# Recurrence of a hybrid attention and RWKV-7 step: another order of ready and late work, key transposes parted from their copies, a solve in five pieces, and bulk loads issued by ScalarE

## The chip, the cores and the metric

The kernel runs on one core of one Trainium2 chip. The metric is the device time of one execution in microseconds, as the median of several runs. Of one more execution there is a profile, taken by the hardware profiler; all rows of the trace that are shown here come from it.

## The reference

One step of a decoder with two layers. Layer 0 is sliding-window attention with sinks, layer 1 is RWKV-7 time mixing. 16 learned meta tokens stand ahead of a prompt of 2048 tokens; eight short samples of four tokens go through the same layers from cached states. The change touches the second layer's recurrence and what follows it. For each head, with a 64x64 state S:

```python
def step(S, inp):
    r_t, w_t, k_t, v_t, a_t, b_t = inp
    sa = jnp.einsum('bhvk,bhk->bhv', S, a_t)
    S = S * w_t[:, :, None, :] + sa[..., None] * b_t[:, :, None, :] + v_t[..., None] * k_t[:, :, None, :]
    return S, jnp.einsum('bhvk,bhk->bhv', S, r_t)
...
y = ((y - mean) * lax.rsqrt(var + GN_EPS)).reshape(B, T, R_WIDTH)
y = y * ln_g.astype(f32) + ln_b.astype(f32)
y = (y + bonus.reshape(B, T, R_WIDTH)) * jax.nn.silu(g.astype(f32))
out = jnp.einsum('btw,wd->btd', y.astype(xn.dtype), w_out)
```

mean and var are those of each head's 64 outputs (a group norm). h + out goes through a last RMS norm and is the result. There are 16 heads.

## The kernel before

The attention comes first, then the projections of the second layer, whose results (decayed r, a, k, b, v and a few small vectors) are written to DRAM. The recurrence is the last third of the time, from about 1640 us on. Its tokens are cut into units: unit 0 holds the meta tokens, units 1 to 16 hold 128 prompt tokens each, in four chunks of 32. The recurrence inside a chunk is solved as a small triangular system, so that only chunks follow one another.

What is done for one chunk (`chain`): TensorE (PE) multiplies L (the a and r vectors, loaded from ar) with Z (the state, and under it the chunk's u and v rows) into C; ScalarE (ACT) copies the upper part to R0s; PE multiplies R0s with TT, the inverse of the chunk's triangular matrix; ACT writes the result, u, into Z; PE multiplies Z with LS (transposed keys) into C, and VectorE (DVE) scales that with the decay pe into the next chunk's Z. That is the only chain through the whole recurrence; its instructions are in rows such as `C<-Z,L`, `R0s<-C`, `C<-R0s,TT`, `Z<-C` and `Z<-C,pe`.

Work for other units is laid around that chain by `steady`, which runs for units 2 to 14. With u the current unit:

- Two units ahead (s): `scores` multiplies BK (keys and b) with L into PSUM pz (`pz<-L,BK`). ACT copies a part of it to LAs, DVE masks the rest into L (`L<-pz,smk`). LAs goes to DRAM (`la_d<-LAs`) and comes back in another layout as LA.
- `inverse`: from LA, GpSimd (POOL) builds X, the triangular inverse, in 31 steps of two operations (`XT<-LA,X`, `X<-X,XT`), with four pieces of steps laid between other work. X goes to DRAM (`tt_d<-X`) and comes back as TT. Units 1 and 2 have their solve on DVE.
- `keys`: PE transposes BK into PSUM kt, ACT copies it to LS (eight copies).
- One unit behind: the group norm of the outputs Y (mean, squares `Y<-ytm`, var, `ytm<-ytm,var`, lng, lnb, then vt, the bonus), then `gate` (pd, gt, transposes yps, yp).
- Two units behind: `project_out` (`po<-wo,yp`), the residual h, the sum of squares, ms on POOL, and the store `out_y_prompt`.

These are generators: `run` lets one go on up to a MARK or for a budget of estimated microseconds. DVE, ACT and POOL are held to the order in which the program states their instructions (`in_order` ties each to the one before). On PE, and on the DMA queue of SyncE (SP), a scheduler places them by priority, between anchors. In the kernel before, every load and store of the recurrence is issued by SP, whose queue is first in, first out: what waits at its head holds all behind it. BK has four buffers (two per unit), L six (two per unit), LAs one, X and LA two each, TT one per parity of the unit, h and ytm one.

The bulk loads of unit s are: BK, two transfers of 512 KB, and four transfers of L, of 256 KB each. They are issued in the first chunk (BK, and L's first half unless it was loaded already), in the second (L's second half) and in the fourth (the first half of the unit after s).

Of the kernel before, what the change touches and what calls it, by code (L numbers as in the profile page):

```python
# [19 lines left out]
P = 128  # L20
# [10 lines left out]
def tile_hybrid_step(ctx: ExitStack, tc: tile.TileContext, a, o, c):  # L31
# [16 lines left out]

    def dma(out, in_):
        return nc.sync.dma_start(out=out, in_=in_).ins  # L50

# [819 lines left out]

    idle = lambda: iter(())
    PRE = min(3, len(units) - 1)
    nbuf = {"L": 6, "BK": 4, "Z": 4}
# [13 lines left out]

    def load_BK(u):
        u.BK, u.L = [], []  # L890
        for half in range(2):
            BK = es.tile([P, 4, 4, 64], F32, name="BK", tag="BK", bufs=nbuf["BK"])
            dma(BK, bk_d[u.blk][:, half * 4:half * 4 + 4, u.c0:u.c0 + u.nch, :])
            u.BK.append(BK)

    def load_L(u, c2):
        L = wl.tile([P, 2, 2, KC, 64], F32, name="L", tag="L", bufs=nbuf["L"])
        w, c0 = min(2, u.nch - 2 * c2), u.c0 + 2 * c2
        for e, ps_ in HS:

            dma(L[ps_, e].rearrange("p c g x -> p (c g x)"), ar_d[u.blk][ps_, c0:c0 + w].rearrange("p c g x -> p (c g x)"))
        return L
# [40 lines left out]
    def scores(u, c2):  # L943

        nch = u.nch
        mk = smk_s if u.kind == "s" else smk
        w = min(2, nch - 2 * c2)
        L = u.L[c2]

        pss = banks(u)  # L950
        for g in range(KC):
            for cc in range(w):
                for e, ps_ in HS:
                    u.scored = mm(pss[e][64 * cc:64 * cc + 64, g, :], u.BK[g // 4][ps_, g % 4, 2 * c2 + cc, :], L[ps_, e, cc, g, :], True, True)
        for cc in range(w):
            r0 = 64 * cc
            for e in range(2):
                la = u.LAs[32 * (1 - e):32 * (1 - e) + 32, :, 2 * c2 + cc]
                sc = pss[e][r0:r0 + 32, :, 0:32].rearrange("p (h g) i -> p h g i", h=2)
                if u.kind == "s":  # L960
                    for half in range(2):
                        tt(v_, la[:, half], sc[:, half], smk_a[r0:r0 + 32, None, :].broadcast_to([32, 4, 32]), ALU.mult)
                else:
                    act(la, sc)
        for cc in range(w):
            r0 = 64 * cc
            for e in range(2):
                tt(v_, L[OS[e], e, cc], pss[e][r0:r0 + 64], mk[r0:r0 + 64, None, :].broadcast_to([64, KC, 64]), ALU.mult)

    def inverse(u, room=None, ln=None):  # L970
# [38 lines left out]
        for j in range(low, 31):  # L1009
            if j in (8, 16, 23):  # L1010
                yield
            w = 3 - j % 4 if u.kind == "s" else 31 - j
            for eng, k0, k1 in cut if w else ():
                ks = slice(max(low // 2, k0), min(j // 2 + 1, k1))
                shape = [P, ks.stop - ks.start, w]
                if shape[1] <= 0:
                    continue
                tt(eng, XT[:, ks, :w], LA[:, j:j + 1, j + 1:j + 1 + w].broadcast_to(shape), X[:, ks, j:j + 1].broadcast_to(shape), ALU.mult)
                tt(eng, X[:, ks, j + 1:j + 1 + w], X[:, ks, j + 1:j + 1 + w], XT[:, ks, :w], ALU.add)
# [15 lines left out]
    with ExitStack() as ph:  # L1035
# [144 lines left out]
        for x, b in enumerate(order):  # L1180
# [39 lines left out]
            if follow is None:  # L1220
# [11 lines left out]
                if nblk > 2:  # L1232
# [3 lines left out]
                    for i, x0, room in ((1, 0, room1), (0, 1024, None)):  # L1236
                        u = us[i]
                        u.LAs = las[:64, x0:x0 + 256 * u.nch].rearrange("p (h c g i) -> p h c g i", h=2, g=4, i=32)
                        for c2 in range(u.np):
                            scores(u, c2)  # L1240
                        for _ in inverse(u, room, las[:, x0 + 1024 - 32:x0 + 1024] if i == 0 else las[:, 1536:1568]):
                            pass
# [19 lines left out]
    with ExitStack() as ph:  # L1262
# [71 lines left out]
        def elementwise(u):  # L1334
# [3 lines left out]
            if u.tt_d is None:  # L1338
                new_LAs(u)
                for c2 in range(u.np):  # L1340
                    scores(u, c2)
# [26 lines left out]
        def keys(u, c2):  # L1368
# [7 lines left out]
            for half in range(2):  # L1376
                hs = slice(half * 4, half * 4 + 4)
                ps = pz.tile([P, 4, 2, 64], F32, name="kt", tag="pz")
                for j in range(4):
                    t_.transpose(out=ps[:w * 64, j].rearrange("p e d -> p (e d)"),  # L1380
                                 in_=u.BK[half][:, j, 2 * c2:2 * c2 + w, :].rearrange("p c x -> p (c x)"), identity=ident)
                for cc in range(w):
                    for e in range(2):
# [93 lines left out]
        def sample_chain(u):  # L1477
# [22 lines left out]
            for gr in range(KC):  # L1500
# [15 lines left out]
                if gr % 2 == 1:  # L1516
                    yield 0.8
            keys(u, 0)
            LS = u.LS[0][0]
# [55 lines left out]
        def group_norm(u):  # L1575
# [12 lines left out]
            for x in range(2):  # L1588
# [16 lines left out]
                yield 2.3  # L1605
            for e in range(2):
# [9 lines left out]
            tt(v_, y, y, bc(var), ALU.mult)  # L1616
            yield 1.1
# [4 lines left out]
            yield 1.1  # L1622
            for e in range(2):
# [30 lines left out]
        def gate_mul(u, ch):  # L1654
# [7 lines left out]
            for j in range(4):  # L1662
                t_.transpose(out=yps[:, j, :], in_=gt[:n, j * P:(j + 1) * P], identity=ident[:n, :n])
            if u.kind == "p":
                yp = wk.tile([P, 2, 4, n], F16, name="yp", tag="yp", bufs=2)
# [59 lines left out]
        for part in range(2):  # L1725
            load_w(0, w_g, "wg", part)
        keys(us[0], 0)
        if len(us) > 1:
            keys(us[1], 0)
        front = sample_all()  # L1730
# [8 lines left out]
        PLAN = {(1, 2): [2], (1, 3): [3], (2, 0): [4], (2, 1): [5], (2, 2): [6], (2, 3): [7]}  # L1739
        side, rests, marked = [], [], []  # L1740
        tails, seen = {}, []
# [14 lines left out]
        def steady(i, u, pe):  # L1756
# [9 lines left out]
            for ch in range(4):  # L1766
# [3 lines left out]
                next(rec)  # L1770
                after_rhs()
                if ch in (1, 2):
                    with released():
                        if ch == 1:
                            new_LAs(s)
                        else:
                            outputs(u, 1)
                        scores(s, ch - 1)
                run(pe[ch], 1.2)
                next(rec)  # L1780
                with released():
                    if ch == 0:
                        if i > 2:
                            keys(u, 1)
                        first = L0s.pop(s.idx, None)
                        load_BK(s)
                        s.L.append(first or load_L(s, 0))
                        small_loads(s)
                    if ch == 1:
                        s.L.append(load_L(s, 1))  # L1790
                    if ch == 3:
                        keys(u.next, 0)
                        if i + 3 < len(us):
                            L0s[i + 3] = load_L(us[i + 3], 0)
                        inv[s.idx] = inverse(s)
                        next(inv[s.idx])
                    elif us[i + 1].idx in inv:
                        next(inv[i + 1], None)
                        if ch == 2:
                            load_TT(us[i + 1])  # L1800
                if ch < 3:
# [19 lines left out]
        def after_rhs():  # L1821

            for gen in list(rests):
                rests.remove(gen)
                if gen in marked:
                    run(gen, to=MARK)
                    marked.remove(gen)
                    rests.append(gen)
                else:
                    run(gen)  # L1830
            with released():
# [4 lines left out]
        def side_work(u, ch, ahead, last):  # L1836
            if u.kind == "p":
                outputs(u, ch)
            if u.next is not None and (u is us[0] or ch == 3):
                keys(u.next, 1)  # L1840
            if u.next is not None and ch == 2:
                keys(u.next, 0)
            next(ahead, None)
# [4 lines left out]
        for i, u in enumerate(us):  # L1848
# [15 lines left out]
            for ch in range(u.nch):  # L1864
# [6 lines left out]
                if i + 1 in inv and i > 1:  # L1871

                    with released():
                        if ch == 0:
                            keys(u, 1)
                        next(inv[i + 1], None)
                        if ch == 2:
                            load_TT(us[i + 1])
                run(ew[ch], 1.2)
# [153 lines left out]
```

## Time and profile before

| | us |
| --- | --- |
| median of 3 runs | 2534.53 |
| lowest, highest run | 2526.64, 2537.41 |
| profiled execution, its time | 2542.64 |
| profiled execution, its span | 2540.9 |
| busy in the span: PE, DVE | 2241.2, 1676.6 |
| busy in the span: ACT, POOL | 1168.9, 1050.7 |

The profiled execution took somewhat longer than the three runs. Its mean granted TensorE clock is 0.949 of full speed. PE is busy for 88% of the span, but a busy PE can run at half its clock or in small matmuls, so that this says little of a single stage. In the recurrence the engines hand work to one another every few microseconds, and the reading goes by the time of one unit and by what each engine waited for in it. In the rows of the timeline and of the waits, a name in brackets behind "<-" is what ended the idle time; "SPq" is the DMA queue of SP, with the time its issues took; a bare "DMA" row is the time from issue to landing, as the chain view shows it. "issue" means that no wait is recorded.

### The profile page before, as it was taken

Reading aid. Unit: us, or ns where it says so; the run is one execution under the profiler, and the core shown is the slowest. Engines: PE = TensorE matmul, PEld = TensorE weight load, DVE = VectorE, ACT = ScalarE, POOL = GpSimd, SP = SyncE. Lnnn points to the kernel's source line nnn. Section 1 sums busy time; section 2 is a strip of 40 time slices with the busy share of each in tenths; the row PEclk is TensorE's granted clock in tenths of the full one; section 3 lists DMA queues with packets and bytes.
Section 4 is the critical chain, followed back from the end, with each engine's and each line's share of the span. In section 5 each row is a group of like instructions: output and inputs, shape, how many; then the busy total and the mean of one; then the engine's idle time right before and its main releaser. Section 6 shows DMA issues by size and latency. Waiting matters only on the chain.

```text
span 2540.9 us, 60840 instructions
## 1 busy us (share of the span) xinstructions
PE 2241.2 (88%) x24932; PEld 1545.2 (61%) x24932; DVE 1676.6 (66%) x3181; ACT 1168.9 (46%) x2799; POOL 1050.7 (41%) x1572
## 2 busy tenths in 40 slices
PE   6999989899999997899999999667888888888897
PEld 5877767667854445477776668345545554555553
DVE  7586683577656987866555666555666676666674
ACT  6676464566432433554433445324445444444431
POOL 4242132233112344443333324324777776777613
PEclk9999998999999998899999999777999999999998
DMA  8433122333247564422222223577355455454423
GB/s 204 127 104 116 60 75 80 109 100 99 87 138 223 196 227 161 137 84 96 88 89 100 88 78 109 146 187 192 104 143 146 119 146 135 121 139 135 103 61 75
DMA packets 346234, 312.97 MB, mean 123 GB/s; under 512 B 205546, under 2 KB 282218, under 8 KB 344131
## 3 DMA queue, kind: packets, MB, share of 16 engines
q1 hardware_dynamic: 344339, 305.30, 41.2%
q0 software_dynamic: 1616, 3.79, 0.7%
q8 instruction: 195, 3.19, 0.5%
q14 instruction: 84, 0.69, 0.1%
HBM read 191.15 MB, written 119.84 MB: 122 GB/s over the span
## 4 chain that ended last, share of the span: by engine, by line
PE 37%; DVE 21%; DMA 15%; ACT 8%; POOL 8%; issue 7%; SPq 4%; POOLq 0%; ACTq 0%; DVEq 0%
PE pd L38 21%; PE po L38 6%; DVE xm L47 5%; SPq L50 4%; PE C L38 3%; DVE xpr L44 2%; DMA TT<-tt_d 2%; DMA BK<-bk 2%; ACT ssb L41 2%; DMA tt_d<-X 2%; POOL X L44 2%; PE pz L38 2%; DMA wst<-in_rwkv_w_in 2%; PE sc L38 1%; POOL XT L44 1%
## 5 line engine op out<-in xcount | busy, mean ns | idle before, releaser
L38 PEld LDWEIGHTS <-yp 128*128 128x128 f16 x1488 | 142.3, 100 | 167.4 <-issue 16.5
L47 DVE SCALAR_TENSOR_TENSOR xm<-dx,mu,xn 128x256 f32<-128x256 f32 (+2 forms) x432 | 200.1, 523 | 49.9 <-POOL dx L44 48.5
L44 POOL TENSOR_TENSOR X<-X,XT 128x126 f32<-128x126 f32 (+24 forms) x458 | 200.9, 439 | 35.6
L44 POOL TENSOR_TENSOR XT<-LA,X 128x126 f32<-128x126 f32 (+24 forms) x458 | 183.6, 401 | 36.2 <-issue 2.5
L38 PE MATMUL pd<-xp,wq 128*128 128x256 f16 (+2 forms) x1728 | 186.1, 266 | 11.8 <-DVE qp L47 8.0
L38 PE MATMUL pd<-wg,xg 128*128 128x512 f16 (+1 forms) x816 | 193.3, 384 | 0.4 <-DMA xg<-xg 0.4
L38 PE MATMUL po<-wo,yp 128*128 128x512 f16 x768 | 193.3, 395 | 0.0
L38 PE MATMUL pd<-xp,wg 128*128 128x256 f16 (+2 forms) x1728 | 187.4, 270 | 0.8 <-DVE xp L44 0.4
L38 PE MATMUL pd<-wvv,xpr 128*128 128x512 f16 (+1 forms) x816 | 186.6, 386 | 0.0
L38 PE MATMUL pd<-xpr,w 128*128 128x256 f16 (+2 forms) x1728 | 186.5, 267 | 0.0
L38 PEld LDWEIGHTS <-wq 128*128 128x128 f16 x1728 | 159.4, 99 | 33.2 <-DVE qp L47 9.2
L38 PE MATMUL pd<-xpr,wkk 128*128 128x256 f16 (+2 forms) x1728 | 179.5, 264 | 0.0
L44 POOL TENSOR_TENSOR ssb<-ssb,bias 128x512 f32<-128x512 f32 x64 | 86.3, 1355 | 222.7 <-DVE ssb L462 181.4
L38 PEld LDWEIGHTS <-wg 128*128 128x128 f16 x1728 | 161.7, 100 | 24.0 <-issue 3.9
L38 PEld LDWEIGHTS <-w 128*128 128x128 f16 x1728 | 157.8, 99 | 27.2 <-issue 9.7
L38 PEld LDWEIGHTS <-wkk 128*128 128x128 f16 x1728 | 158.2, 98 | 15.6 <-issue 0.4
L38 PE MATMUL pd<-w,yp 128*128 128x512 f16 x720 | 162.2, 383 | 3.5 <-DMA yp<-y 3.5
L44 POOL TENSOR_TENSOR ps<-wst,ps 128x1024 f16<-128x1024 f32 x32 | 69.4, 2170 | 226.8 <-ACT wst L41 208.3
L44 DVE TENSOR_TENSOR L<-pz,smk 64x512 f32<-64x512 f32 x128 | 88.1, 689 | 96.7 <-ACT LAs L41 94.7
L38 PEld LDWEIGHTS <-xpr 128*128 128x128 f16 (+1 forms) x816 | 78.8, 100 | 102.1 <-issue 16.4
L44 DVE TENSOR_TENSOR xpr<-xm,xpr 128x512 f16<-128x512 f32 (+2 forms) x144 | 99.0, 709 | 56.7 <-ACT xpr L41 56.3
L41 ACT ACTIVATE ssb<-ssb,ng 128x128 f32<-128x128 f32 (+1 forms) x272 | 104.2, 384 | 57.3 <-DVE es L44 53.6
(357 smaller groups left out, 4715.4 us busy)
## 6 DMA issues: line engine op xcount, KB each, us to landing
wst<-in_rwkv_w_in SPq DMA_DIRECT2D x32, 512.0 KB
wsp<-ps SPq DMA_DIRECT2D x32, 512.0 KB
BK<-bk SPq DMA_DIRECT2D x32, 512.0 KB
L<-ar SPq DMA_DIRECT2D x64, 256.0 KB
x<-in_x_prompt SPq DMA_DIRECT2D x29, 512.0 KB
xn<-xn SPq DMA_DIRECT2D x14, 1028.0 KB
ar<-aro SPq DMA_DIRECT2D x28, 512.0 KB
bk<-bko SPq DMA_DIRECT2D x28, 512.0 KB
```

The costliest lines, as they stand in the source:

```text
L38: return t_.matmul(out=out, lhsT=lhsT, rhs=rhs, start=start, stop=stop, **kw).ins
L41: return s_.activation(out=out, in_=in_, func=func, **kw).ins
L44: return e.tensor_tensor(out=out, in0=in0, in1=in1, op=op).ins
L47: v_.scalar_tensor_tensor(out=out, in0=in0, scalar=scalar, in1=in1, op0=op0, op1=op1)
L50: return nc.sync.dma_start(out=out, in_=in_).ins
```

## The change

Four things are changed, all of them in the recurrence.

1. In `steady`, the work of a chunk is stated in another order: norm's next step is stated ahead of the masking of L, the rests of gate and project_out are taken in reverse order up to a MARK, and of some the remainder comes a chunk later.
2. `scores` and `keys` become generators: `scores` yields between the copies to LAs and the masking into L, and `keys` between the transposes and the copies. In the fourth chunk the transposes are stated ahead of the solve's matmuls.
3. BK and L are loaded through ScalarE's DMA queue, behind the state update: in the first chunk BK and all that is missing of L, in the fourth the first half of L for the unit after.
4. `inverse` is cut at steps 8, 16, 22 and 26, into five pieces (before: 8, 16 and 23). One piece is taken early in the third chunk, and load_TT is stated behind the state update.

The core of the diff:

```diff
-    def dma(out, in_):
-        return nc.sync.dma_start(out=out, in_=in_).ins
+    def dma(out, in_, eng=None):
+        return (eng or nc.sync).dma_start(out=out, in_=in_).ins
...
-        for cc in range(w):
-            r0 = 64 * cc
-            for e in range(2):
+        yield
+        for e in range(2):
+            for cc in range(w):
+                r0 = 64 * cc
                 tt(v_, L[OS[e], e, cc], pss[e][r0:r0 + 64], mk[r0:r0 + 64, None, :].broadcast_to([64, KC, 64]), ALU.mult)
...
-            if j in (8, 16, 23):
+            if j in (8, 16, 22, 26):
                 yield
...
                 rec = chain(u, ch)
                 next(rec)
-                after_rhs()
+                left = rests[::-1]
+                del rests[:]
+                with released():
+                    if ch == 2:
+                        next(inv.get(i + 1, idle()), None)
+                for gen in left:
+                    run(gen, to=MARK)
+                with released():
...
+                    if ch in (1, 2):
+                        sc = scores(s, ch - 1)
+                        next(sc)
+                    if ch == 3:
+                        kt = keys(u.next, 0)
+                        next(kt)
+                if ch < 3:
+                    run(norm, to=MARK)
+                if ch == 2:
+                    rests.extend(left)
+                else:
+                    for gen in left:
+                        run(gen)
                 if ch in (1, 2):
                     with released():
-                        if ch == 1:
-                            new_LAs(s)
-                        else:
-                            outputs(u, 1)
-                        scores(s, ch - 1)
+                        all_of(sc)
...
                 next(rec, None)
+                with released():
+                    if ch == 0:
+                        first = L0s.pop(s.idx, None)
+                        load_BK(s, s_)
+                        s.L.append(first or load_L(s, 0, s_))
+                        s.L.append(load_L(s, 1, s_))
+                        small_loads(s)
+                    if ch == 2 and i + 1 in inv:
+                        load_TT(us[i + 1])
+                    if ch == 3 and i + 3 < len(us):
+                        L0s[i + 3] = load_L(us[i + 3], 0, s_)
                 run(pe[ch], to=MARK)
                 rests.append(pe[ch])
-                if ch == 1 and i > 2:
-                    marked.append(pe[ch])
```

What this does to the order on three engines follows. The columns are the line, the operation, output and inputs, the tile's shape and a count. First DVE in the second chunk of a steady unit, before (h is the residual of two units behind, po its projection):

```order
L44 TENSOR_TENSOR Z_19046<-C,pe 64x256 x4
L47 SCALAR_TENSOR_TENSOR h_27641<-po,h_27641 128x512
L44 TENSOR_TENSOR L<-pz,smk 64x512 x4
L44 TENSOR_TENSOR ytm<-ytm,var 128x1024
L44 TENSOR_TENSOR ytm<-ytm,lng 128x1024
L44 TENSOR_TENSOR Z_19047<-C,pe 64x256 x4
```

and after:

```order
L44 TENSOR_TENSOR Z_19046<-C,pe 64x256 x4
L47 SCALAR_TENSOR_TENSOR h_27644<-po,h_27644 128x512
L44 TENSOR_TENSOR ytm<-ytm,var 128x1024
L44 TENSOR_TENSOR L<-pz,smk 64x512 x4
L44 TENSOR_TENSOR ytm<-ytm,lng 128x1024
L44 TENSOR_TENSOR Z_19047<-C,pe 64x256 x4
```

`ytm<-ytm,var`, the first step of the norm's end, has moved ahead of the four maskings of L. In the third chunk `ytm<-ytm,lnb` moves likewise.

Second ACT in the first chunk and at the start of the second, before (`po,ssq` is the sum of squares of the residual):

```order
L41 ACTIVATE Y_22359<-ytm 128x512
L41 ACTIVATE Y_22722<-ytm 128x512
L41 ACTIVATE R0s<-C 128x256
L41 ACTIVATE po,ssq_22756<-h_22755 128x512
L41 ACTIVATE LAs<-pz 32x2x128 x4
L41 ACTIVATE Z_19046<-C 32x256 x4
```

and after:

```order
L41 ACTIVATE Y_22365<-ytm 128x512
L41 ACTIVATE Y_22719<-ytm 128x512
L50 DMA BK<-bk_148 128x4x256 x2
L50 DMA L<-ar_157 64x1024 x2
L41 ACTIVATE R0s<-C 128x256
L41 ACTIVATE po,ssq_22759<-h_22758 128x512
L41 ACTIVATE LAs<-pz 32x2x128 x4
L41 ACTIVATE Z_19046<-C 32x256 x4
```

Four DMA issues, two of BK and two of L, now stand between the squares and R0s, on the engine that copies R0s.

Third SP, from the load of L in the second chunk to the loads of TT, before (ln, pe and bont are small vectors, c_laneid is the identity with which X begins):

```order
L50 DMA L<-ar_161 64x1024 x2
L50 DMA ln<-ln_195 64x32 x2
L50 DMA la_d<-LAs 32x32x32 x2
L50 DMA X<-c_laneid 128x512
L50 DMA Z_19046<-v_114 32x512
L50 DMA pe<-pe_178 128x32
L50 DMA bont<-bo_214 128x16
L50 DMA LA<-la_d 64x1024 x2
L50 DMA tt_d<-X 64x16x32 x2
L50 DMA vt<-v_113 128x512 x2
L50 DMA TT<-tt_d 64x1x512 x2
```

and after:

```order
L50 DMA ln<-ln_195 64x32 x2
L50 DMA X<-c_laneid 128x512
L50 DMA Z_19046<-v_114 32x512
L50 DMA la_d<-LAs 32x32x32 x2
L50 DMA pe<-pe_178 128x32
L50 DMA bont<-bo_214 128x16
L50 DMA tt_d<-X 64x16x32 x2
L50 DMA LA<-la_d 64x1024 x2
L50 DMA vt<-v_113 128x512
L50 DMA TT<-tt_d 64x1x512 x2
L50 DMA vt<-v_113 128x512
```

L has left the queue, `tt_d<-X` stands ahead of `LA<-la_d`, and the second load of vt stands behind TT's.

More of the change, by code (lines that the diff above doesn't have):

```diff
@@ L872, in tile_hybrid_step, with all_of @@
     idle = lambda: iter(())
+    def all_of(gen):
+        for _ in gen:
+            pass
     PRE = min(3, len(units) - 1)
@@ L887, in begin, with load_BK @@
         return u
-    def load_BK(u):
+    def load_BK(u, eng=None):
         u.BK, u.L = [], []
@@ L892, in load_BK, with load_L @@
             BK = es.tile([P, 4, 4, 64], F32, name="BK", tag="BK", bufs=nbuf["BK"])
-            dma(BK, bk_d[u.blk][:, half * 4:half * 4 + 4, u.c0:u.c0 + u.nch, :])
+            dma(BK, bk_d[u.blk][:, half * 4:half * 4 + 4, u.c0:u.c0 + u.nch, :], eng)
             u.BK.append(BK)
-    def load_L(u, c2):
+    def load_L(u, c2, eng=None):
         L = wl.tile([P, 2, 2, KC, 64], F32, name="L", tag="L", bufs=nbuf["L"])
@@ L899, in load_L @@
         for e, ps_ in HS:
-            dma(L[ps_, e].rearrange("p c g x -> p (c g x)"), ar_d[u.blk][ps_, c0:c0 + w].rearrange("p c g x -> p (c g x)"))
+            dma(L[ps_, e].rearrange("p c g x -> p (c g x)"), ar_d[u.blk][ps_, c0:c0 + w].rearrange("p c g x -> p (c g x)"), eng)
         return L
@@ L964, in scores @@
                     act(la, sc)
-        for cc in range(w):
-            r0 = 64 * cc
-            for e in range(2):
+        yield
+        for e in range(2):
+            for cc in range(w):
+                r0 = 64 * cc
                 tt(v_, L[OS[e], e, cc], pss[e][r0:r0 + 64], mk[r0:r0 + 64, None, :].broadcast_to([64, KC, 64]), ALU.mult)
@@ L1239, in tile_hybrid_step @@
                         for c2 in range(u.np):
-                            scores(u, c2)
+                            all_of(scores(u, c2))
                         for _ in inverse(u, room, las[:, x0 + 1024 - 32:x0 + 1024] if i == 0 else las[:, 1536:1568]):
@@ L1340, in elementwise @@
                 for c2 in range(u.np):
-                    scores(u, c2)
+                    all_of(scores(u, c2))
                     next(load, None)
@@ L1375, in keys @@
                 LScount[0] += 2
-            for half in range(2):
-                hs = slice(half * 4, half * 4 + 4)
-                ps = pz.tile([P, 4, 2, 64], F32, name="kt", tag="pz")
+            pss = [pz.tile([P, 4, 2, 64], F32, name="kt", tag="pz") for _ in range(2)]
+            for half, ps in enumerate(pss):
                 for j in range(4):
@@ L1381, in keys @@
                                  in_=u.BK[half][:, j, 2 * c2:2 * c2 + w, :].rearrange("p c x -> p (c x)"), identity=ident)
+            yield
+            for half, ps in enumerate(pss):
+                hs = slice(half * 4, half * 4 + 4)
                 for cc in range(w):
@@ L1517, in sample_chain @@
                     yield 0.8
-            keys(u, 0)
+            all_of(keys(u, 0))
             LS = u.LS[0][0]
@@ L1604, in group_norm @@
                            mean[ps_, x * 8:x * 8 + 8].unsqueeze(2).broadcast_to([64, 8, 64]), ALU.subtract)
-                yield 2.3
+                yield MARK if vts and x == 0 else 2.3
             for e in range(2):
@@ L1616, in group_norm @@
             tt(v_, y, y, bc(var), ALU.mult)
-            yield 1.1
+            yield MARK
             yf = u.ytm[:n]
@@ L1621, in group_norm @@
             tt(v_, yf, yf, lnb[:n], ALU.add)
-            yield 1.1
+            yield MARK
             for e in range(2):
@@ L1663, in gate_mul @@
                 t_.transpose(out=yps[:, j, :], in_=gt[:n, j * P:(j + 1) * P], identity=ident[:n, :n])
+            yield MARK
             if u.kind == "p":
@@ L1726, in tile_hybrid_step @@
             load_w(0, w_g, "wg", part)
-        keys(us[0], 0)
+        all_of(keys(us[0], 0))
         if len(us) > 1:
-            keys(us[1], 0)
+            all_of(keys(us[1], 0))
         front = sample_all()
@@ L1739, in tile_hybrid_step @@
         PLAN = {(1, 2): [2], (1, 3): [3], (2, 0): [4], (2, 1): [5], (2, 2): [6], (2, 3): [7]}
-        side, rests, marked = [], [], []
+        side, rests = [], []
         tails, seen = {}, []
@@ L1770, in steady @@
                 next(rec)
-                after_rhs()
+                left = rests[::-1]
[6 more added lines that the diff above has]
+                with released():
+                    for fn in side:
+                        fn()
+                    del side[:]
+                    if ch == 1:
+                        new_LAs(s)
+                    if ch == 2:
+                        outputs(u, 1)
+                    if ch in (1, 2):
[6 more added lines that the diff above has]
+                    run(norm, to=MARK)
+                if ch == 2:
+                    rests.extend(left)
+                else:
+                    for gen in left:
+                        run(gen)
                 if ch in (1, 2):
                     with released():
-                        if ch == 1:
-                            new_LAs(s)
-                        else:
-                            outputs(u, 1)
-                        scores(s, ch - 1)
+                        all_of(sc)
                 run(pe[ch], 1.2)
@@ L1781, in steady @@
                 with released():
[L1782 to L1790, printed above, removed]
+                    if ch == 0 and i > 2:
+                        all_of(keys(u, 1))
                     if ch == 3:
-                        keys(u.next, 0)
-                        if i + 3 < len(us):
-                            L0s[i + 3] = load_L(us[i + 3], 0)
+                        all_of(kt)
                         inv[s.idx] = inverse(s)
                         next(inv[s.idx])
[L1797 to L1800, printed above, removed]
+                    else:
+                        next(inv.get(i + 1, idle()), None)
                 if ch < 3:
@@ L1821, in after_rhs @@
         def after_rhs():
[L1823 to L1830, printed above, removed]
+            for gen in rests:
+                run(gen)
+            del rests[:]
             with released():
@@ L1839, in side_work @@
             if u.next is not None and (u is us[0] or ch == 3):
-                keys(u.next, 1)
+                all_of(keys(u.next, 1))
             if u.next is not None and ch == 2:
-                keys(u.next, 0)
+                all_of(keys(u.next, 0))
             next(ahead, None)
@@ L1874, in tile_hybrid_step @@
                         if ch == 0:
-                            keys(u, 1)
+                            all_of(keys(u, 1))
                         next(inv[i + 1], None)
                         if ch == 2:
+                            next(inv[i + 1], None)
                             load_TT(us[i + 1])
```

## The prediction

> **What bounds the kernel now.** I read the page's chain first, then the time of one period of the recurrence, the list of waits over ten periods, and last the timeline of one unit, engine by engine. All instructions ahead of unit 2's recurrence stand as before, so only the stretch from about 1640 us to the end is in question. The chain by engine:
>
> ```profile
> PE 37%; DVE 21%; DMA 15%; ACT 8%; POOL 8%; issue 7%; SPq 4%; POOLq 0%; ACTq 0%; DVEq 0%
> ```
>
> No engine alone carries it; it hops. So I take ten steady units: the first matmuls of the second chunk of unit and unit (start, us, engine, idle before), and the busy time in the window between (sum, PE, PEld, DVE, ACT, POOL, granted clock, DMA share, GB/s).
>
> ```profile
> 1827.78 0.65 PE L38 MATMUL C<-Z,L 128*32 128x64 f32 x32 [1.07 <-issue]
> 2307.53 0.65 PE L38 MATMUL C<-Z,L 128*32 128x64 f32 x32 [0.71 <-PE po L38]
> 1828.00:2308.00 480.00, 406.38 (x7631) 247.24 (x7619) 316.18 (x501) 212.18 (x540) 342.10 (x691) 0.95 0.53 135
> ```
>
> (2307.53 − 1827.78)/10 = 47.98 us per unit, PE busy 40.6 of it and POOL 34.2. The waits in that window (sum, count, longest):
>
> ```profile
> PE C L38 <- issue: 33.6, 25, 1.6
> POOL LA L44 <- DMA LA<-la_d: 31.8, 10, 4.9
> POOL ms L1694 <- ACT po L41: 28.1, 10, 4.8
> POOL var L1613 <- DVE var L1610: 27.7, 10, 4.3
> PE C L38 <- DMA TT<-tt_d: 21.9, 13, 2.5
> PE pz L38 <- DMA BK<-bk: 3.5, 7, 0.8
> ```
>
> PE waits for DVE (the "issue" rows stand where Z is being scaled) and 2.19 us per unit for TT, the end of POOL's solve. POOL's three waits are 8.76 per unit, so its own loop needs 39.2 beside them. These are two coupled loops: PE's, with some 7 us of gaps, and POOL's, which runs X, tt_d, TT on one side and la_d, LA on the other.
>
> **Part 1, ready work ahead of late (DVE).** In chunk 1 of one unit:
>
> ```profile
> 2165.39 2.79 DVE L44 TENSOR_TENSOR L<-pz,smk 64x512 f32<-64x512 f32 x4 [2.76 <-ACT LAs L41]
> 2168.11 1.15 PE L38 MATMUL C<-Z,LS 128*64 128x64 f32 x32
> 2168.21 1.25 DVE L44 TENSOR_TENSOR ytm<-ytm,var 128x1024 f32<-128x1024 f32 x1
> 2170.82 1.73 DVE L44 TENSOR_TENSOR Z<-C,pe 64x256 f32<-64x256 f32 x4
> 2172.65 0.65 PE L38 MATMUL C<-Z,L 128*32 128x64 f32 x32 [1.33 <-issue]
> 2183.82 0.65 PE L38 MATMUL C<-Z,L 128*32 128x64 f32 x32 [1.30 <-issue]
> ```
>
> DVE idles 2.76 us ahead of L, and then puts ytm<-ytm,var (1.25) between L and Z. Moved into the idle stretch it costs nothing there, and Z starts 1.25 earlier, at 2169.57, still behind the state matmuls' end (2168.11 + 1.15 = 2169.26). PE's gap of 1.33 closes; in chunk 2 ytm<-ytm,lnb moves likewise, gap 1.30. Together −2.63 per unit. It is covered as long as LAs comes as late as now; were it 1.25 earlier, ytm would push L back, and the gap would stay.
>
> **Part 2, keys parted (PE).** The eight transposes now stand ahead of the solve's matmuls in the fourth chunk:
>
> ```profile
> 2185.03 0.94 PE L38 MATMUL C<-R0s,TT 32*32 32x64 f32 x32 [0.55 <-ACT R0s L41]
> ```
>
> PE waits 0.55 there for R0s, which the transposes fill: −0.55. Bounds: 0 to −0.55; I take the latter since BK lies ready by then.
>
> **Part 3, BK and L issued by ACT.** Per unit two BK and four L issues leave SP. Today:
>
> ```profile
> 2155.38 0.97 SPq L50 DMA_DIRECT2D BK<-bk  x2
> 2155.90 7.51 DMA BK<-bk
> 1870.86 6.30 DMA BK<-bk
> 1720.37 8.21 DMA BK<-bk
> 2163.46 0.69 PE L38 MATMUL pz<-L,BK 64*64 64x64 f32 x32 [0.18 <-DMA BK<-bk]
> 2158.24 1.10 ACT L41 ACTIVATE Y<-ytm 128x512 f32<-128x512 f32 x2
> 2162.77 0.38 ACT L41 ACTIVATE R0s<-C 128x256 f32<-128x256 f32 x1 [3.44 <-PE C L38]
> ```
>
> The second BK was issued at 2155.90 and landed 7.51 later; PE wanted it at 2163.28. ACT reaches the issue only behind the squares, at 2159.34, so the second goes out at 2159.83 and lands 6.30 to 7.51 later, 2166.1 to 2167.3: a wait of 2.85 to 4.06 where 0.18 was, +2.7 to +3.9. That scores' wait also costs what stands behind it, since PE runs slower after a wait:
>
> ```profile
> 2164.09 1.47 PE L38 MATMUL po<-wo,yp 128*128 128x512 f16 x6
> 2066.01 1.13 PE L38 MATMUL pz<-L,BK 64*64 64x64 f32 x32 [0.76 <-DMA BK<-bk]
> 2067.08 2.49 PE L38 MATMUL po<-wo,yp 128*128 128x512 f16 x6
> ```
>
> The same six matmuls took 1.47 after a short wait and 2.49 after one of 0.76: +1.02.
>
> [...]
>
> The issues themselves: ACT pays 2×0.49 for BK and 4×0.55 for L (the price on SP of LA, below, 1.09 for two) = 3.2 us per unit. The first four, 2.1, fit in the 3.44 ahead of R0s; the last two, 1.1, in ACT's idle 1.08 ahead of gt, at the turn from the fourth chunk to the next unit:
>
> ```profile
> 2195.15 0.60 ACT L41 ACTIVATE gt<-pd 128x512 f32<-128x512 f32 x1 [1.08 <-PE pd L38]
> ```
>
> Taken as 0. With that cover gone they delay R0s, and PE with it, by their own length; the upper bound of one issue is the held one on SP, 2.32 (next part).
>
> [...]
>
> **Part 4, five solve pieces, tt_d ahead of LA.** POOL and SP around the turn from one solve to the next:
>
> ```profile
> 2175.61 0.37 POOL L44 TENSOR_TENSOR XT<-LA,X 128x96 f32<-128x96 f32 x1
> 2178.25 0.33 POOL L44 TENSOR_TENSOR XT<-LA,X 128x70 f32<-128x70 f32 x1
> 2180.18 2.32 SPq L50 DMA_DIRECT2D X<-c_laneid  x1
> 2183.46 1.27 POOL L44 TENSOR_TENSOR X<-X,ln 128x512 f32<-128x512 f32 x1
> 2184.21 1.09 SPq L50 DMA_DIRECT2D LA<-la_d  x2
> 2185.34 1.34 SPq L50 DMA_DIRECT2D tt_d<-X  x2
> 2186.78 2.91 SPq L50 DMA_DIRECT2D vt<-v  x2
> 2189.60 1.92 POOL L44 TENSOR_TENSOR LA<-LA,ln 128x1024 f32<-128x1024 f32 x1 [4.86 <-DMA LA<-la_d]
> 1991.37 1.09 SPq L50 DMA_DIRECT2D LA<-la_d  x2
> 1996.00 1.92 POOL L44 TENSOR_TENSOR LA<-LA,ln 128x1024 f32<-128x1024 f32 x1 [2.56 <-DMA LA<-la_d]
> 2199.05 1.06 PE L38 MATMUL C<-R0s,TT 32*32 32x64 f32 x28 [2.21 <-DMA TT<-tt_d]
> ```
>
> The step pieces 12 to 14 now stand ahead of ms's small operations, so that 2178.25 − 2175.61 = 2.64 us of the solve falls into the ms wait (2.81 per unit). X ends and tt_d goes out that much earlier, more than the 2.19 that PE waits for TT: −2.19. Late next is LA. X ends at 2183.46 + 1.27 = 2184.73. LA, now issued behind tt_d, waits for X, and SP's queue is first in, first out: tt_d's 1.34 and a tenth, 1.45, then LA. The transfer behind a pair on scratch memory is held: vt behind tt_d took 2.91 where two issues take about 1.1, and X<-c_laneid behind la_d 2.32; so a hold of 2.0. From LA's issue to POOL's start took 2189.60 − 2184.21 = 5.39 here, 1996.00 − 1991.37 = 4.63 there. From X's end to LA in use: low 1.45 + 4.63 = 6.08, taken 1.45 + 2.0 + 4.63 = 8.08, high 1.45 + 2.0 + 5.39 = 8.84. It was 4.87 in this unit and 3.18 in the mean (31.8 over ten). With 39.2 of other work, POOL's loop is 45.3, 47.3 or 48.0. I take the middle, because the two held rows stand right behind such stores.
>
> **Sum.** PE's loop: 47.98 − 2.63 − 0.55 − 2.19 = 42.61; plus 2.7 to 3.9 and 1.02: 46.3 to 47.5. POOL's: 47.3. The period is the longer, about 47.3: 0.7 less per unit. Twelve units (3 to 14) have their solve on POOL and a steady turn: −8.4 us. Unit 2, where ACT's L issues may wait behind the last weight loads, −3 to +4, taken 0. The profiled execution took 2542.64, so 2534.2; the median shown, 2534.53, is 8.1 below that execution, and less 8.4 is **2526**.
>
> **Rivals.**
> A larger gain: LA is not held (6.08) and the slow matmuls fall away. Period 46.3 to 45.3, −20 to −32 us: 2502 to 2514. For it speaks that POOL then has 8.76 us of waits to lose; against it both held rows.
> Slower: BK arrives too late. At the 8.21 of the third row it lands at 2168.04, a wait of 4.76: 42.61 + 4.58 + 1.02 = 48.2, and if one issue on ACT is held like 2.32 instead of 0.49, 50.0: +3 to +25 us, 2537 to 2559. It decides from a landing of about 7.8 us after the second issue on. For it: PE stands still, so all of DVE's gain is spent waiting. Against: only one of three rows is that long.
> No change: POOL's loop at 8.84 gives 48.0, and what DVE and PE gain turns into waiting for TT: 2534 ± 4.
>
> **How the numbers follow.** The runs spread from 2526.64 to 2537.41, so 0.5%, 12.7 us, is about what can be told from no change: under 2521.9 is faster, over 2547.2 slower. Forecast 0.38 (a third of it beyond 12.7 by the low bounds: 0.13 faster, 0.25 same); larger gain 0.26, all faster; no change 0.16 (0.03 slower, for holds I haven't counted); slower 0.20 (0.13 beyond). Faster 0.39, same 0.45, slower 0.16. The range leaves out the forecast's neighbours' ends only: 2502 (the lowest of the larger gain) to 2550 (the middle of the slower case).
>
> **What would show it.** Part 1: no "issue" wait of 1.3 ahead of chunks 2 and 3, and DVE's ytm<-ytm,var in the former idle stretch. Part 3: PE's wait for BK up from 0.35 to about 3 us per unit, and slow po behind it; a row near zero would move the sum to the larger gain. Part 4: TT's wait gone, LA's wait near 6 to 8 us, ms's wait near 0. The prediction is wrong if ACT's issues take over 1 us each, or if TT's wait stays at 2 us.

## The result, and the profile after

The changed kernel took 2601.01 us (median of 4 runs, 2596.79 to 2605.12) against 2533.4 for the kernel before (median of 4 runs): a ratio of 1.027, 95% interval 1.0241 to 1.0298. It is slower by some 68 us, where 2526 was forecast. The profiled execution took 2601.98 us (2542.64 before). Of the experiments below, one execution of run 5 (9062.43 us) and one of run 8 (3772.41 us) were far slower than their other three, and the medians given leave them out.

The chain by engine on the page, and the same window of the recurrence (sum, PE, PEld, DVE, ACT, POOL, granted clock, DMA share, GB/s):

```profile
PE 50%; DVE 18%; issue 10%; ACT 9%; DMA 8%; POOL 4%; SPq 2%; POOLq 0%; ACTq 0%; DVEq 0%
1828.00:2308.00 480.00, 365.73 (x6862) 226.33 (x6859) 294.90 (x451) 191.68 (x488) 305.89 (x621) 0.89 0.48 121
```

Nine units pass in it where there were ten, and the granted clock is 0.89 instead of 0.95. The period, from the second chunk's first matmuls, is (2365.60 − 1831.64)/10 = 53.4 us against 47.98:

```profile
1831.64 0.65 PE L38 MATMUL C<-Z,L 128*32 128x64 f32 x32 [1.07 <-issue]
2365.60 0.65 PE L38 MATMUL C<-Z,L 128*32 128x64 f32 x32 [1.55 <-issue]
```

The waits of that window (sum, count, longest):

```profile
PE C L38 <- issue: 105.5, 18, 11.8
DVE vt L44 <- DMA vt<-v: 90.4, 18, 7.7
POOL LA L44 <- DMA LA<-la_d: 65.4, 9, 7.6
PE pz L38 <- DMA BK<-bk: 4.3, 5, 1.3
```

The new row is DVE's wait for vt: 90.4 us over nine units, 10.0 per unit. In the kernel before, the same row of the same window was small, and the prediction did not show it:

```profile
DVE vt L44 <- DMA vt<-v: 4.9, 6, 1.1
```

PE's wait for TT is gone, and so are the "issue" gaps ahead of the third and fourth chunk. The gap ahead of the second chunk stays (1.07 and 1.55 in the rows above), and a new one, of 9.0 to 11.8 us, stands in each unit at the turn to the next. SP's and ACT's queues, DVE and PE there:

```profile
2065.28 1.35 SPq L50 DMA_DIRECT2D tt_d<-X  x2
2066.73 2.32 SPq L50 DMA_DIRECT2D LA<-la_d  x2
2069.11 0.58 SPq L50 DMA_DIRECT2D vt<-v  x1
2070.39 1.09 SPq L50 DMA_DIRECT2D TT<-tt_d  x2
2071.57 0.38 SPq L50 DMA_DIRECT2D vt<-v  x1
2071.49 0.46 ACTq L50 DMA_DIRECT2D L<-ar  x1
2073.13 1.97 DVE L44 TENSOR_TENSOR vt<-vt,bont 128x512 f32<-128x512 f32 x1 [2.91 <-DMA vt<-v]
2082.16 0.86 DVE L44 TENSOR_TENSOR vt<-vt,bont 128x512 f32<-128x512 f32 x1 [7.06 <-DMA vt<-v]
2082.95 1.72 DVE L44 TENSOR_TENSOR Z<-C,pe 64x256 f32<-64x256 f32 x4
2071.23 1.15 PE L38 MATMUL C<-Z,LS 128*64 128x64 f32 x32
2084.77 1.08 PE L38 MATMUL C<-Z,L 128*32 128x64 f32 x32 [10.33 <-issue]
```

The first vt load was in use 4.0 us after its issue (2069.11 to 2073.13). The second, issued at 2071.57 behind the two TT loads, was in use 10.6 us after (2082.16). DVE's order is fixed, and behind that vt stands the scaling of Z, whose matmuls had ended at 2072.38. So PE stood for 10.33 us, and it started again at a slower pace: 1.08 for the 32 matmuls that take 0.65, at a granted clock of 0.50 from 2084.70 to 2086.70.

### The profile page after: what moved, and what is told of

Same layout as the page of the kernel before. It is cut to its first block, busy times and chain, and to the rows that moved or that the text cites. A ratio compares the mean times of both kernels' runs of the same rounds, so it can differ in the third digit from the quotient of the medians.

```text
span 2600.2 us, 60852 instructions
## 1 busy us (share of the span) xinstructions
PE 2238.5 (86%) x24932; PEld 1547.7 (60%) x24932; DVE 1687.0 (65%) x3181; ACT 1169.5 (45%) x2799; POOL 1044.8 (40%) x1572
## 4 chain that ended last, share of the span: by engine, by line
PE 50%; DVE 18%; issue 10%; ACT 9%; DMA 8%; POOL 4%; SPq 2%; POOLq 0%; ACTq 0%; DVEq 0%
PE pd L38 29%; PE po L38 5%; PE C L38 5%; DVE xm L47 4%; DMA BK<-bk 2%; DVE xpr L44 2%; ACT ssb L41 2%; PE pz L38 2%; SPq L50 2%; PE Y L38 2%; PE sc L38 1%; PE oT L38 1%; DMA wst<-in_rwkv_w_in 1%; DMA L<-ar 1%; PE kt L1385 1%
## 5 line engine op out<-in xcount | busy, mean ns | idle before, releaser
L38 PE MATMUL C<-Z,L 128*32 128x64 f32 x2048 | 49.5, 247 | 170.4 <-issue 159.9
L38 PE MATMUL pd<-xp,wq 128*128 128x256 f16 (+2 forms) x1728 | 186.0, 266 | 11.4 <-DVE qp L47 8.0
L38 PEld LDWEIGHTS C<-Z,L 128*32 128x32 f32 x2048 | 38.9, 126 | 195.8 <-issue 192.3
L41 ACT ACTIVATE R0s<-C 128x256 f32<-128x256 f32 x65 | 25.0, 385 | 274.9 <-PE C L38 269.9
```

The costliest lines, as they stand in the source:

```text
L38: return t_.matmul(out=out, lhsT=lhsT, rhs=rhs, start=start, stop=stop, **kw).ins
L41: return s_.activation(out=out, in_=in_, func=func, **kw).ins
```

## The experiments

Two theories were to be told apart. A: the second vt load is late because of its place behind TT. B: it is late because ACT's L loads run in the same microseconds. Behind them stood the question what bounds the kernel once vt is in time. In the code, "..." stands for lines that are not shown. Behind each time stand its ratio to the kernel before and the 95% interval of that ratio.

**1. Both vt loads ahead of TT.** All other engines' orders as in the changed kernel.

```diff
...
                     norms_[u.idx] = group_norm(u)
                     run(norms_[u.idx], to=MARK)
+                    if i + 1 in inv:
+                        with released(), tc.issue_after(last["vt"]):
+                            load_TT(us[i + 1])
                     run(norms_[u.idx], to=MARK)
...
-                    if ch == 2 and i + 1 in inv:
-                        load_TT(us[i + 1])
```

> The changed kernel with one thing moved: both loads of vt stand ahead of the two TT loads in SP's queue (tt_d x2, LA x2, vt x2, TT x2); the order of all other engines is as in the changed kernel. Theory A (place in the queue): DVE's second vt load waits behind TT's transfer of small pieces, 7 us per unit, and Z's scaling waits behind DVE. Then the wait of 7.06 falls to 0 to 2 us, the period falls from 53.3 to 46 to 47.5 us and the time from 2601 to 2510-2540 us. Theory B (contention: the L loads that ACT issues in the same microseconds slow vt's transfer): the wait stays near 7 us, 2590-2610 us.

2544.46 us (1.0042 of before, 1.0026 to 1.0058): 57 us of the 68 come back when the second vt load changes places with TT's two.

```profile
DVE vt L44 <- DMA vt<-v: 25.1, 10, 3.4
POOL LA L44 <- DMA LA<-la_d: 76.7, 10, 9.3
PE C L38 <- DMA TT<-tt_d: 22.4, 11, 3.7
PE pz L38 <- DMA BK<-bk: 11.2, 9, 2.2
```

DVE's wait for vt falls from 10.0 to 2.5 us per unit, and all of that stands ahead of the first of the two loads. So it went as A said, though the time ended 4 us above its range. This run alone doesn't rule out B, since vt now also goes out ahead of ACT's L loads (2044.90 and 2047.03 in one unit); runs 4 and 6 part the two. TT's wait is back with 2.2 per unit, and POOL waits 7.7 for LA.

**2. vt ahead of the solve's last piece.** SP's queue then reads LA, vt x2, tt_d x2, LA, TT x2.

```diff
...
-                else:
+                if ch == 2:
                     norms_[u.idx] = group_norm(u)
                     run(norms_[u.idx], to=MARK)
+                    with released(), tc.issue_after(last["vt"]):
+                        next(inv.get(i + 1, idle()), None)
+                if ch == 3:
...
```

> The changed kernel with both loads of vt stated ahead of the solve's last piece, so that SP's queue reads LA, vt x2, tt_d x2, LA, TT x2. Theory A: both waits of DVE for vt go (2.91 and 7.06 us per unit), period 43.5 to 46 us, 2490-2525 us; late next is LA on POOL or BK on PE. Theory B: vt is issued about 6 us ahead of the L loads, so it is no longer slowed by them either, and this run alone doesn't tell A from B; it gives the price of the whole wait.

2562.72 us (1.0121, 1.0081 to 1.0161). A miss: vt's wait is nearly gone, but what is put behind it is late instead.

```profile
DVE vt L44 <- DMA vt<-v: 1.7, 2, 1.1
POOL LA L44 <- DMA LA<-la_d: 92.2, 10, 11.2
PE C L38 <- DMA TT<-tt_d: 52.0, 19, 3.6
```

**3. The bulk loads issued by SP again.**

```diff
-                        load_BK(s, s_)
+                        load_BK(s)
```

(and L's loads likewise)

> The changed kernel with the BK and L loads issued by SP again, at the same places of the program; the second vt load still stands behind TT. Theory A: DVE's wait for the second vt stays at 6 to 8 us per unit, 2585-2615 us. Theory B: with no loads of ACT beside it, vt lands early, its wait falls to 0 to 2 us, 2520-2545 us.

2534.16 us (1.0003, 0.9985 to 1.0022). The expectation was wrong in its premise: with the loads on SP the scheduler puts the second vt load ahead of TT, so the run doesn't tell A from B. Its queue reads tt_d x2, vt, LA x2, vt, TT x2, with the first vt load ahead of LA as well. DVE still waits 4.3 us per unit for vt:

```profile
DVE vt L44 <- DMA vt<-v: 43.4, 20, 3.1
```

Its period, (2294.07 − 1820.98)/10 = 47.31 us, is the one that was forecast, while its median is that of the kernel before. Run 6 repeats the run with the second vt load held behind TT.

**4. The kernel before with the second vt load behind TT.** Nothing else moves on any engine.

```diff
...
-                    dma(vt.rearrange("p g d -> p (g d)"), v_d[u.t][u.cols, e, :])
+                    nx = getattr(u, "next", None)
+                    behind = getattr(nx, "TT_in", None) if e == 1 and u.idx > 2 else None
+                    with tc.issue_after(behind) if behind is not None else ExitStack():
+                        dma(vt.rearrange("p g d -> p (g d)"), v_d[u.t][u.cols, e, :])
```

> The kernel before with one thing moved: the second vt load of each steady unit stands behind the two TT loads in SP's queue; no other engine's order changes, and ACT issues nothing. Theory A: DVE gets a wait of 5 to 7 us per unit for it; 2.2 us of that lie beside PE's wait for TT, so the time rises by 12 x 3 to 12 x 6 us, to 2570-2605 us. Theory B: no change, 2526-2542 us.

2586.43 us (1.0211, 1.0179 to 1.0244), in the range that A gave, with a wait of about 7.5 us for the second vt, a little more than A said. This place in the queue alone costs 52 us, without any load on ACT:

```profile
DVE vt L44 <- DMA vt<-v: 70.6, 16, 7.6
PE C L38 <- issue: 87.7, 27, 8.3
2053.99 1.11 SPq L50 DMA_DIRECT2D TT<-tt_d  x2
2055.20 0.38 SPq L50 DMA_DIRECT2D vt<-v  x1
2062.72 0.69 DVE L44 TENSOR_TENSOR vt<-vt,bont 128x512 f32<-128x512 f32 x1 [7.55 <-DMA vt<-v]
```

**5. LA and vt ahead of tt_d, in the changed kernel** (la_d stated right behind the scores, the solve's last piece behind vt).

```diff
...
-                else:
+                if ch == 2:
+                    with released():
+                        next(inv[s.idx])
                     norms_[u.idx] = group_norm(u)
-                    run(norms_[u.idx], to=MARK)
+                    with tc.issue_after(s.la_in):
+                        run(norms_[u.idx], to=MARK)
+                    with released(), tc.issue_after(last["vt"]):
+                        next(inv.get(i + 1, idle()), None)
+                if ch == 3:
...
```

> The changed kernel with SP's queue in the order la_d x2, LA x2, vt x2, tt_d x2, TT x2 (la_d stated right behind the scores; before it tt_d stood ahead of LA and one vt behind TT). Theory C (with vt ahead of TT, POOL's loop bounds through LA behind tt_d): POOL's wait for LA falls from 7.7 us (first run of this study) to 3 to 5.5 us, DVE's wait for vt to under 1 us; period 43.5 to 46 us, 2480-2515 us. Theory D (what bounds the run with vt ahead of TT is the BK loads on ACT's queue, which come too late for PE): LA's shorter wait brings nothing, POOL waits elsewhere, 2535-2550 us.

2565.68 us (1.0117, 1.008 to 1.0154). LA's wait fell to 4.6 us per unit as C said, and yet the time is 21 us above run 1's: TT, now last, is waited for 4.6 us per unit. Neither theory gave that.

```profile
POOL LA L44 <- issue: 46.0, 10, 6.2
PE C L38 <- DMA TT<-tt_d: 45.9, 18, 4.2
```

**6. Bulk loads on SP, and the second vt load held behind TT.** The edits of runs 3 and 4 together, on the changed kernel.

```diff
-                        load_BK(s, s_)
+                        load_BK(s)
...
-                    dma(vt.rearrange("p g d -> p (g d)"), v_d[u.t][u.cols, e, :])
...
+                    with tc.issue_after(behind) if behind is not None else ExitStack():
+                        dma(vt.rearrange("p g d -> p (g d)"), v_d[u.t][u.cols, e, :])
```

> The changed kernel with BK and L issued by SP and the second vt load held behind TT (in the run with the bulk loads on SP, the scheduler had put it ahead of TT). Theory A (place behind TT): DVE's wait for the second vt is 6 to 8 us per unit again, 2575-2610 us. Theory B (contention with ACT's L loads): the wait stays at the 2 us of that run, 2526-2545 us.

2572.32 us (1.0158, 1.012 to 1.0195): just below the 2575 that A gave, far above B's 2545. DVE waits for the second vt again, 8.11 and 8.02 us in two units and 8.4 at most; from its issue to its use 8.2 us pass in one unit (2105.04 to 2113.22), where 10.6 passed in the changed kernel, with ACT's L loads beside it:

```profile
DVE vt L44 <- DMA vt<-v: 90.3, 19, 8.4
```

So the changed kernel and three runs form a square: vt early and the loads on SP 2534 (run 3), vt late on SP 2572 (run 6), vt early and the loads on ACT 2544 (run 1), vt late on ACT 2601 (the changed kernel). The late place costs 38 or 57 us, the loads on ACT 10 or 29; each makes the other dearer. In both runs on SP the first vt load also stands ahead of LA, so that the 10 and 29 contain what that brings. A is the main cause, B a part.

**7. The kernel before with only the bulk loads on ACT.**

```diff
-                        first = L0s.pop(s.idx, None)
-                        load_BK(s)
-                        s.L.append(first or load_L(s, 0))
-                        small_loads(s)
...
                 next(rec, None)
+                with released():
+                    if ch == 0:
+                        first = L0s.pop(s.idx, None)
+                        load_BK(s, s_)
+                        s.L.append(first or load_L(s, 0, s_))
+                        s.L.append(load_L(s, 1, s_))
+                        small_loads(s)
+                    if ch == 3 and i + 3 < len(us):
+                        L0s[i + 3] = load_L(us[i + 3], 0, s_)
```

> The kernel before with only the BK and L loads moved to ACT's queue, at the places that the change gives them; vt x2 stays ahead of TT, the order of DVE, ACT's arithmetic and POOL stays. By the prediction's part 3: PE's wait for BK rises from 0.35 to 3 to 4 us per unit and po behind it gets slower by 1 us, 12 x 1.5 to 12 x 4 us more (part hidden under the wait for TT): 2550-2580 us. Rival: BK comes in time, since PE wants it later than the trace of one unit says, and the loads cost nothing: 2526-2542 us.

2593.57 us (1.023, 1.019 to 1.0271). Dearer than expected, and not through BK (2.0 us of waiting over the whole window). One thing that the trace shows is L's loads meeting TT's:

```profile
PE pz L38 <- DMA BK<-bk: 2.0, 2, 1.0
PE C L38 <- issue: 57.8, 26, 10.5
PE C L38 <- DMA TT<-tt_d: 22.5, 12, 4.3
2014.77 1.12 SPq L50 DMA_DIRECT2D TT<-tt_d  x2
2015.67 0.45 ACTq L50 DMA_DIRECT2D L<-ar  x1
2025.26 1.07 PE L38 MATMUL C<-R0s,TT 32*32 32x64 f32 x28 [4.27 <-DMA TT<-tt_d]
```

TT was in use 10.5 us after its first issue where the kernel before needed 8.1 (2190.95 to 2199.05); there L went out behind that. In the next unit it was 10.6 us (2066.73 to 2077.30). In the kernel before it was 8.1 to 8.9 over the window's units in which PE waited for TT. So with L's loads beside it TT took some 2 us longer.

But the 57 us are not explained by that. Over the whole window PE waits for TT no longer than before (22.5 us against 21.9); what grows most are its "issue" gaps, from 33.6 to 57.8. The run differs in more than ACT's issues: in two of the twelve steady units the scheduler put both vt loads behind TT, and PE stood for 10.5 and 4.9 us at the turn there; and on PE half of the second chunk's scores stand behind the first matmuls of the solve in every unit. How the 57 us divide was not settled.

**8. The kernel before with only DVE's order in the second and third chunk.**

```diff
...
-                        scores(s, ch - 1)
+                        sc = scores(s, ch - 1)
+                        next(sc)
+                    run(norm, to=MARK)
+                    with released():
+                        all_of(sc)
```

> The kernel before with only DVE's order of the second and third chunk changed: ytm<-ytm,var and ytm<-ytm,lnb ahead of the four maskings of L. By the prediction's part 1 PE's gaps of 1.33 and 1.30 us close and the period falls by up to 2.6 us: 2503-2520 us. Rival: POOL's solve bounds, what is gained is waited for at TT (2.2 us per unit rises to 4 or more): 2528-2540 us.

2529.3 us (0.9969, 0.9928 to 1.001): the rival by the time, though TT's wait rose to 2.6 us per unit only. The gaps shrink, and most of the gain is waited for elsewhere.

```profile
PE C L38 <- issue: 19.6, 15, 1.9
POOL LA L44 <- DMA LA<-la_d: 47.0, 10, 5.8
PE C L38 <- DMA TT<-tt_d: 26.3, 17, 2.6
DVE vt L44 <- DMA vt<-v: 18.7, 10, 3.0
```

Against before, "issue" is 14.0 us less over ten units, LA 15.2 more, vt 13.8 more, TT 4.4 more.

**9. Run 1 with L's last two loads moved behind the solve that waits for TT.**

```diff
+                    if ch == 0:
+                        first = load_L(s, 0, s_)
                     if ch == 0 and i > 2:
                         all_of(keys(u, 1))
...
-                    if ch == 3 and i + 3 < len(us):
-                        L0s[i + 3] = load_L(us[i + 3], 0, s_)
```

> The run with both vt loads ahead of TT (2544 us), with one thing more: the two L loads that ACT issues at the end of the fourth chunk, in the same microseconds in which TT and vt are under way, are issued in the next unit's first chunk instead, behind the solve that waits for TT. Theory E (what ACT's L loads cost is the collision with TT and vt): TT lands 1 to 2 us earlier after its issue, DVE's wait for vt falls from 2.5 to about 1 us, the time to 2515-2535 us. Rival F (ACT's loads cost in another place: BK and its issues on ACT, or nothing): 2540-2555 us, the more so as L now comes late for the scores.

2536.24 us (0.9997, 0.9979 to 1.0016), just above E's range. The collision was real: PE has no wait for TT left in the window, and vt's falls to 0.9 us per unit. In run 1 TT was in use 11.4 to 12.4 us after its first issue in three units; here it was in time 8.5 us after it in one (1996.80 to 2005.29). But now BK, issued behind L, is late. As in run 7, half of the second chunk's scores moved behind the first matmuls of the solve, so that more than L's place differs from run 1.

```profile
DVE vt L44 <- DMA vt<-v: 9.1, 7, 2.3
PE pz L38 <- DMA BK<-bk: 26.9, 11, 3.6
POOL LA L44 <- DMA LA<-la_d: 75.5, 10, 9.0
```

**10. The same move in run 7** (the code is set against run 7's).

```diff
                     if ch == 0:
+                        first = load_L(s, 0, s_)
                         if i > 2:
                             keys(u, 1)
...
-                    if ch == 3 and i + 3 < len(us):
-                        L0s[i + 3] = load_L(us[i + 3], 0, s_)
```

> The kernel before with the bulk loads on ACT (2594 us), with the same one thing more: the two L loads of the fourth chunk issued in the next unit's first chunk, behind the solve. Theory E: the landing of TT goes back from 10 to 8 us, the long waits for vt (11 us at the worst) go, 2540-2560 us. Rival F: 2585-2605 us.

2599.23 us (1.0254, 1.0232 to 1.0276). By the number rival F, and yet E's collision is gone:

```profile
PE C L38 <- DMA TT<-tt_d: 3.2, 3, 1.8
```

PE's wait for TT falls from 22.5 to 3.2 us, and the time does not follow: BK is late as in run 9 (21.2 us over ten waits), and the scheduler put both vt loads behind TT in three of the twelve steady units. So the run does not settle where run 7's 57 us lie.

**11. Run 9 with LA ahead of tt_d.**

```diff
...
-                        next(inv.get(i + 1, idle()), None)
+                        if ch == 2:
+                            next(inv[s.idx])
+                        with tc.issue_after(s.la_in) if ch == 2 else ExitStack():
+                            next(inv.get(i + 1, idle()), None)
...
```

> The run with vt ahead of TT and L's loads behind the solve (2536 us), with LA's loads ahead of tt_d in SP's queue, as in the kernel before (la_d, LA x2, tt_d x2, vt x2, TT x2). In that run POOL waits 7.6 us per unit for LA and 1.9 for ms, and PE waits for TT not at all. Theory G (POOL's way from X to LA is what bounds now): LA's wait falls to 3 to 5 us, the period from 47.5 to 44.5-46 us, 2500-2520 us. Theory H (tt_d and TT come later by what LA gains, PE waits for TT again, as in the run with LA and vt ahead of tt_d): 2530-2555 us.

2553.1 us (1.0063, 1.004 to 1.0086): theory H; PE waits for TT again, 19.8 us over ten units, while POOL's wait for LA fell to 5.4 us per unit only.

**12. Bulk loads on SP, LA, tt_d, vt, TT in the order of before.** Of the change DVE's order, the parted keys and the five pieces are left. To run 1's edit come:

```diff
...
+                        with tc.issue_after(s.la_in) if ch == 2 else ExitStack():
+                            next(inv.get(i + 1, idle()), None)
...
-                        load_BK(s, s_)
+                        load_BK(s)
...
```

> The changed kernel with the bulk loads on SP, vt ahead of TT and LA ahead of tt_d (before's order of these), so that of the change DVE's order, the parted keys and the five pieces are left. In the run with the bulk loads on SP (2534 us) POOL waited 8.2 us per unit for LA and DVE 4.6 for vt, and PE for neither TT nor BK. Theory G: LA's wait falls to 3 to 5 us, 2500-2520 us. Theory H: TT's wait comes back with 2 to 3 us per unit, 2525-2545 us.

2526.68 us (0.9963, 0.995 to 0.9977): theory H by the time and by TT's 2.6 us per unit, and the only version of this study that is clear of noise below the kernel before, by 0.4%. POOL's wait for LA, with the three times that tt_d's store ended it, is 5.2 us per unit.

```profile
POOL LA L44 <- DMA LA<-la_d: 36.9, 7, 7.1
POOL LA L44 <- DMA tt_d<-X: 14.8, 3, 5.1
PE C L38 <- DMA TT<-tt_d: 25.9, 15, 2.7
DVE vt L44 <- DMA vt<-v: 23.0, 10, 3.7
```

## Why the prediction was wrong

**The step that failed** is part 4's. It followed tt_d, LA and TT through SP's queue and priced the hold on the transfer behind tt_d, but counted vt only as a witness for that hold. The order it was made from shows the second vt load behind TT, and the sum has no term for it, nor for Z's scaling behind it on DVE: vt's place was priced at nothing, without a reason. Measured: 10.0 us per unit of waiting for vt where 0.5 stood, and 57 us that come back with the second load's place (run 1); the place alone costs 52 in the kernel before (run 4) and 38 with the bulk loads on SP (run 6 against run 3). The slower rival had the right sign and the wrong mechanism, BK. (By its own terms it sets in at a landing of 8.0 us, not 7.8.) Of the signs that the prediction named, those of part 1 and part 4 all came, and neither of its two signs of being wrong did; the time was 75 us off through a load that the list does not hold.

**Part 1** was right in its place: ahead of the third and fourth chunk hardly a gap is left in the changed kernel. As a gain it was mis-sized: alone it brought 0.3%, not clear of nothing (run 8), since vt, LA and TT became late instead.

**Part 2**: R0s's wait ahead of the solve is gone in the changed kernel; its own worth was not run, nor that of the five pieces alone.

**Part 3** failed in its mechanism. BK's wait, forecast at 2.85 to 4.06 us, was 0.48 per unit (4.3 over nine), 1.1 in run 1:

```profile
2040.34 0.37 ACTq L50 DMA_DIRECT2D BK<-bk  x1
2040.75 0.84 ACTq L50 DMA_DIRECT2D BK<-bk  x1
2041.39 0.58 ACT L41 ACTIVATE Y<-ytm 128x512 f32<-128x512 f32 x1
2047.69 0.69 PE L38 MATMUL pz<-L,BK 64*64 64x64 f32 x32 [1.26 <-DMA BK<-bk]
2048.32 1.47 PE L38 MATMUL po<-wo,yp 128*128 128x512 f16 x6
```

The landing was as counted: the second BK was in use 6.9 us after its issue. What was wrong is when ACT issues it. The prediction let the issue wait until the squares (`Y<-ytm`) were done, as the program's order has it; in the trace the first issue starts about 1.05 us ahead of the first square, in all nine units of the window. So PE wanted the second BK 5.7 us after its issue (at 2047.69 less its wait of 1.26), where 3.45 had been counted. The slower clock behind it seldom came either: the six matmuls of po took 1.47 us here after a wait of 1.26, at a granted clock of 1.00, and 2.72 in one unit of nine, at 0.53 behind a wait of 0.67. The cost lay where the prediction put none: ACT's L issues take little of ACT's time (0.45 to 0.84 us each), but the loads run beside TT and vt. In the changed kernel's order the loads on ACT cost 10 us with vt early and 29 with vt late; run 7's 57 contains more than them.

**Part 4's sizes**: from X's end to LA in use 8.08 was taken, between 6.9 and 7.6 was measured in the changed kernel. POOL's wait for LA was 7.3 us per unit there, 7.7 in run 1, so that term held; and ms's wait is gone, as foreseen. TT's wait did not vanish by the earlier X alone: it is back in run 1 with 2.2, and absent again in run 9, where L's loads no longer run beside TT.

## What to carry to other kernels

When a queue is first in, first out, price every transfer that changes its neighbour, not only those the change speaks of: a load that was waited for 0.5 us per unit cost 52 us when it was put behind two others. Follow the load to its consumer, and ask what stands behind the consumer on an engine whose order is fixed. And where several short loops share one queue, moving one transfer ahead makes another late (runs 2, 5 and 11): the gain of an engine's better order must be sought in all of their waits.

## What the runs showed of the hardware

The time of one and the same load from issue to use changed with what stood ahead of it in the queue and beside it: vt, 256 KB, took 4.0 us behind LA and 10.6 behind TT in one unit of the changed kernel, and 7.5 behind TT without ACT's loads beside it (run 4, 2055.20 to 2062.72). I had not expected that the next load would take so long behind two of 128 KB each.

SP issued its transfers one behind another: in the changed kernel tt_d's stores went out at 2065.28, as X ended (2065.26), and LA's loads, which stand behind them in the queue, at 2066.73, although the last of la_d's stores had been issued by 2062.63.

A DMA issue on ACT's queue did not wait for the ACTIVATE instructions stated ahead of it: in the changed kernel it started 1.05 us before the first of the two squares that the program states ahead of it (2040.34 and 2041.39). The trace shows this in nine units out of nine; what lets the issue run ahead was not looked into.
